# Score, level and first accumulator pairs in two-bank tiles, with two banks each for projections and the rest, in a hybrid mixer kernel

## The chip, the cores and the metric

The kernel runs on one core of a Trainium2 chip. The metric is the device time of one execution in microseconds. Three runs of the kernel before gave 436.5, 437.03 and 437.03 us, so the median is 437.03 us.

## The reference

One layer works on 128 context rows and 512 latent rows, 640 rows of width 1024 in all. They are RMS-normalised, scaled and shifted by vectors that come from a conditioning product, and sent through one input projection. The projected columns feed three groups of heads, each of which is multiplied by a SiLU gate. Then come one output projection, an RMSNorm, a gate and the residual. Cut to what matters here:

```python
h = rmsnorm(x, g_pre) * (1 + scale) + shift          # scale, shift, gate = silu(c) @ w_ada + b_ada
qa, ka, va, ga, qr, zf, zb, ir, gr, uf, gf = split(h @ w_in)
# A: 8 heads of 64; a latent row reads its 8 x 16 window and 256 cached context keys, with a bias
s = concat([q @ k_window.T * scale + bias, q @ k_ctx.T * scale])
oa = softmax(s) @ concat([v_window, v_ctx])
# B: 4 heads of 64, forward and backward gated recurrence, written in chunks
o = (q * exp(G)) @ state + (decayed q @ k.T, causal) @ v
# C: Re(2-D DFT over positions and group channels) @ w_fnet
mixed = concat([oa * silu(ga), rmsnorm(o_r) * silu(gr), o_f * silu(gf)])
y = x + gate * rmsnorm(mixed @ w_out, g_post)
```

## The kernel before

Everything is laid out with columns of the model on the partitions and the 640 rows along the free side. Products in 32-bit precision are made as three products of a high and a low part (`split`, lines 126 to 128, writes a high part on ScalarE and a low part on VectorE).

The stages are generators, each of which yields when it would wait, and a small clock (`Order`, lines 39 to 68) interleaves them into one program. The framework then schedules that program against a simulated time line (`TCKW`, line 36). For each engine it takes, of the instructions whose inputs and buffers are ready, the one that stands earliest in the program. The order that comes out is fixed at build time, and on the chip each engine works through its own list and waits on semaphores. `issue_after` and `add_manual_dep` add edges that keep one instruction behind another.

The stages around the change are these.

- **Start** (`start_stream`, 242 to 279; `zf_stream`, 281 to 292). For each of eight k, `mod_cols` (192 to 198) makes 16 small products with 32 output columns each, in four column groups, into a tile `pm`. They are turned by `tr`, summed, and give scale and shift; `modulated` (231 to 240) turns the rows of x into the tile `px` and applies them. The projections `zf0` and `zf1` run along as the k arrive, into four accumulators `zf_acc` (206), and `gate` (319 to 327) reads them.
- **Projections** (`block`, 297 to 312). Each of the other blocks of 128 columns is made in two halves of 320 rows. One half is 24 products of 320 columns into one accumulator `acc`, which a `use` function then reads on ScalarE or VectorE. The block `ir` is made by `token_blocks` (348) with products of 256 columns.
- **Recurrence** (`recurrence`, 414 to 551), twice. Seven levels each make, in `level` (431 to 450), eight and then two products of 64 contraction rows. The two heads of a pair sit on the upper and the lower 64 rows, and their products alternate between two accumulators `pa`. VectorE copies them out under a mask (450). After the levels come the tiles `pd`, `pk`, `pst` and the two output accumulators `po` (529).
- **Attention** (`attention`, 637 to 776), four times, each with four latent tiles and one context tile. `scores` (641 to 647) makes a run of products of 64 contraction rows. In a latent tile that is six against the cached keys (names `kc` and `tqs`) and six against the window's keys (`tks` and `tqs`), alternating between two accumulators `pss`, one for each head of the pair. In the context tile it is six of 128 columns. The softmax, the turned probabilities (`transposes`, tile `ptr`), and the weighted sums (`weighted`, `context_rest`) follow.
- **Gate vectors** (`gate_vectors`, 844 to 876). Eight times 8 products through `mod_cols` into `pm`, read by a `split`, and four times four products into `pg`, read on VectorE in line 875.
- **Fourier and output** (`fourier`, 798; `out_first`, 895; `out_second`, 919). Five accumulators `pz`, then `pf`, then the output projection over four banks at once and one more, then its second half.

PSUM has eight accumulator tiles ("banks" here) of 512 columns. `PB(tag)` (105) takes one from a tag: `b` has five and `f` three (`WB`, 27). Projections take `f`, as do the single-bank part of `by_token` (343), `pm` and `pg` of the gate vectors, `pz`, `pf`, `pw` and the second half of the output projection. All else takes `b`. Of `zf_acc` three banks are `f` and one is `b`. The first half of `zb0` takes `b`.

The alternating order of a run is held by `follow` (115 to 120): every product of a run gets an edge to the one before it. The edge keeps the order, but lets other products in between. The two accumulators of a pair are two tiles, and a product can be scheduled when its own tile is free:

```python
pss, pes, chain = [PB(), PB()], [], []
...
for hh in (1, 0):
    follow(chain, mm(outs[hh], qs[a][RS[hh], cols], keys(b)[RS[hh]], start=(n == 0), stop=(n == 2)))
```

Of the kernel before, what the change touches and what calls it, by code (L numbers as in the profile page):

```python
# [9 lines left out]
F32 = mybir.dt.float32  # L10
# [7 lines left out]
P = 128  # L18
# [8 lines left out]
WB = {"raw": 2, "hi": 3, "lo": 3, "t": 18, "pe": 2, "o": 4, "cf": 3, "pb": 5, "pf": 3, "s": 8, "m": 4, "row": 2, "tbl": 1, "pT": 8, "vs": 2, "kc": 4}  # L27
# [44 lines left out]
def mixer_kernel(ctx: ExitStack, tc: tile.TileContext, A, O):  # L72
# [34 lines left out]

    last_tr = [None]
# [6 lines left out]
    def follow(chain, ins):  # L115

        if chain:
            tc.add_manual_dep(ins, chain[-1].name, mybir.DependencyInfo(mybir.DependencyClass.NoSync,
                                                                        mybir.DependencyReason.DATA), reason="turns")
        chain.append(ins)  # L120
# [71 lines left out]
    def mod_cols(out, w):  # L192

        t = od.now
        for k in range(KT):
            o = out[32 * (k % 4):32 * (k % 4) + 32, :]
            mm(o, csil[:, k, :], w[:, k, :], start=(k < 4), stop=(k >= 4))
        od.now = t + 0.45
# [7 lines left out]
    zf_w, zf_acc = [], [[PB("f"), PB("f")], [PB("f"), PB()]]  # L206
# [35 lines left out]
    def start_stream():  # L242
# [13 lines left out]
        for k in range(KT):  # L256
# [3 lines left out]
            pm = PB()  # L260
            for u in range(2):
                mod_cols(pm[:, u * P:(u + 1) * P], raws[2 * k + u])
# [34 lines left out]
    def block(name, use, lo_eng=ve):  # L297

        w = load_w(A["win"][BLOCKS.index(name)], lo_eng)
        for u in range(2):  # L300
            acc = PB("bf"[u] if name == "zb0" else "f")[:, 0:320]
# [112 lines left out]
    def recurrence(p):  # L414
# [16 lines left out]
        def level(KB, QB, li):  # L431
# [3 lines left out]
            for i0, i1 in ((0, 4), (4, 5)):  # L435
                pa = [PB(), PB()]
                t, chain = od.now, []
                for i in range(i0, i1):
                    for hh in (1, 0):
                        ins = mm(pa[hh][:, (i - i0) * P:(i - i0 + 1) * P], KB[RS[hh], i * P:(i + 1) * P],  # L440
                                 QB[RS[hh], i * P:(i + 1) * P])
                        follow(chain, ins)
# [86 lines left out]
        po = PB(), PB()  # L529
# [107 lines left out]
    def attention(p):  # L637
# [3 lines left out]
        def scores(outs, qt, keys, chain):  # L641

            cols, t = slice(qt * P, (qt + 1) * P), od.now
            for n, (a, b) in enumerate(((0, 0), (0, 1), (1, 0))):
                for hh in (1, 0):
                    follow(chain, mm(outs[hh], qs[a][RS[hh], cols], keys(b)[RS[hh]], start=(n == 0), stop=(n == 2)))
# [4 lines left out]
        def softmax_context():  # L651
            pss, pes = [PB(), PB()], []
# [16 lines left out]
        def softmax_latent(qt):  # L669
            pss, pes, chain = [PB(), PB()], [], []  # L670
# [127 lines left out]
    def fourier():  # L798
# [28 lines left out]
        for u in range(2):  # L827
            pf = PB("f"), PB("f")
# [15 lines left out]
    def gate_vectors():  # L844
        selr = cp.tile([P, 2, P], F32R, tag="selr", name="selr")
        gp.tensor_copy(selr, sel)
        for q in range(8):
# [16 lines left out]
            mod_cols(pm[:, 0:P], w)  # L864
# [30 lines left out]
    def out_first():  # L895
# [8 lines left out]
        banks = [PB() for _ in range(4)]  # L904
# [7 lines left out]
        banks.append(PB("b" if WB["pb"] > 4 else "f"))  # L912
# [216 lines left out]
```

## Time and profile before

| | before |
|---|---|
| median of 3 runs | 437.03 us |
| the profiled execution's own time | 437.11 us |
| its span | 435.3 us |
| granted TensorE clock, mean over the span | 0.996 |
| VectorE busy | 303.5 us (70%) |
| ScalarE busy | 205.8 us (47%) |
| mean DMA rate | 109 GB/s |

The span goes from the first to the last instruction of one execution on the chip, and 1.8 us of that execution's time lie outside it. In the views, PE is TensorE's products, PEld its weight loads, DVE is VectorE and ACT is ScalarE. A row of the time line gives the start, the length of the stretch, the engine, the line, what is written and read, the shape and the count. Products overlap in TensorE's pipeline, so what a product costs is the step from its start to the next one's start, and not its length. An accumulator has the name `pb`, whatever its tag. A product of 64 contraction rows shows as 64*128, and one of `mod_cols` as 128*32. A full 32-bit product shows as two instructions.

### The profile page before, as it was taken

How to read it: one execution, taken by the hardware profiler on the slowest of the kernel's cores; microseconds unless marked ns; L12 is line 12 of the kernel's file. 1: busy time of each engine (PE TensorE's matmuls, PEld its weight loads, DVE VectorE, ACT ScalarE, POOL GpSimd, SP SyncE). 2: the span in 40 equal slices, each digit the busy share in tenths (PEclk: the TensorE clock that was granted, in tenths of full speed). 3: DMA queues.
4: the chain of work that ended last, by engine and by line, in shares of the span. 5: the costliest groups of instructions: out<-in, count | busy, mean ns of one | idle time of the engine just before them, and what ended most of it. 6: DMA issues, size and time to landing. Idle time of an engine off the chain costs nothing.

```text
span 435.3 us, 8309 instructions
## 1 busy us (share of the span) xinstructions
PE 411.3 (94%) x3176; PEld 372.7 (86%) x3176; DVE 303.5 (70%) x866; ACT 205.8 (47%) x546; POOL 7.4 (2%) x23
## 2 busy tenths in 40 slices
PE   0699999999998999999999999999999999999994
PEld 0488899999988998999899889889898988988884
DVE  2775479999986866885597658885768928670174
ACT  6434467565341526654444444753556643350161
POOL 2000000000020100000000000000000000000000
PEclk9999999999999999999999999999999999999998
DMA  7996153211302021122021413245134302481023
GB/s 236 412 407 229 49 158 114 74 45 50 88 20 76 10 62 48 56 97 74 32 68 60 145 50 104 98 147 163 51 119 150 96 0 66 140 291 48 0 105 139
DMA packets 19528, 47.62 MB, mean 109 GB/s; under 512 B 3184, under 2 KB 6912, under 8 KB 19488
## 3 DMA queue, kind: packets, MB, share of 16 engines
q1 hardware_dynamic: 19376, 46.94, 32.0%
q8 instruction: 25, 0.41, 0.4%
q0 software_dynamic: 112, 0.14, 0.3%
q14 instruction: 15, 0.12, 0.1%
HBM read 43.80 MB, written 3.28 MB: 108 GB/s over the span
## 4 chain that ended last, share of the span: by engine, by line
PE 90%; DVE 3%; DMA 3%; ACT 1%; issue 1%; SPq 0%; DVEq 0%; ACTq 0%
PE pb L113 84%; PE pb L124 7%; DMA vs<-wss 2%; DMA txa<-x 1%; DVE AL L450 1%; DVE t L524 1%; DVE AL L487 0%; ACT L679 0%; DVE t L951 0%; ACT pe L680 0%; DVE t L467 0%; DVE t L466 0%; DVE AC L450 0%; DVE t L468 0%; SPq L190 0%
## 5 line engine op out<-in xcount | busy, mean ns | idle before, releaser
L113 PE MATMUL pb<-hT,hi 128*128 128x320 f32 x896 | 208.7, 317 | 2.5 <-DVE vs L128 1.5
L113 PEld LDWEIGHTS pb<-hT,hi 128*128 128x128 f32 x896 | 148.7, 188 | 9.0 <-issue 3.3
L113 PE MATMUL pb<-hT,lo 128*128 128x320 f32 x448 | 139.1, 312 | 0.0
L113 PEld LDWEIGHTS pb<-hT,lo 128*128 128x128 f32 x448 | 84.0, 188 | 1.3 <-DVE G L272 0.2
L128 DVE TENSOR_TENSOR lo<-raw,hi 128x1024 fp32r<-128x1024 f32 x35 | 42.8, 1223 | 18.7 <-ACT hi L127 18.5
L127 ACT CAST hi<-raw 128x1024 fp32r<-128x1024 f32 x35 | 36.8, 1050 | 28.4 <-PE pb L113 17.5
L113 PE MATMUL pb<-t,t 64*128 64x128 f32 (+2 forms) x414 | 42.9, 291 | 0.4 <-DVE AL L450 0.4
L113 PEld LDWEIGHTS pb<-t,t 64*128 64x128 f32 (+1 forms) x414 | 36.0, 188 | 4.7 <-issue 0.7
L127 ACT CAST pT<-pb 128x256 fp32r<-128x256 f32 x64 | 23.5, 373 | 22.3 <-DVE pT L128 11.1
L113 PE MATMUL pb<-hi,mh 128*128 128x512 f32 (+1 forms) x108 | 30.8, 375 | 0.0
L128 DVE TENSOR_TENSOR pT<-pb,pT 128x256 fp32r<-128x256 f32 x64 | 26.5, 419 | 1.7 <-ACT pT L127 1.5
L679 ACT ACTIVATE pe<-pb,s 128x256 f32<-128x256 f32 x32 | 15.3, 478 | 17.5 <-DVE s L678 8.4
L113 PEld LDWEIGHTS pb<-hi,mh 128*128 128x128 f32 x108 | 19.6, 188 | 3.7 <-DVE mh L128 0.3
L113 PE MATMUL pb<-pT,mh 128*128 128x512 f32 (+1 forms) x102 | 21.9, 364 | 0.0
L124 PE MATMUL pb<-ident,pe 128*128 128x128 f32 x136 | 21.0, 274 | 0.5 <-ACT pe L680 0.5
L113 PEld LDWEIGHTS pb<-pT,mh 128*128 128x128 f32 x102 | 17.7, 189 | 3.1
L113 PE MATMUL pb<-lo,mh 128*128 128x512 f32 (+1 forms) x54 | 19.5, 375 | 0.0
L934 ACT ACTIVATE t<-pb 128x512 f32<-128x512 f32 (+1 forms) x11 | 6.1, 552 | 26.9 <-PE pb L113 26.7
L690 DVE TENSOR_TENSOR o<-pb,o 64x512 f32<-64x512 f32 (+1 forms) x16 | 7.8, 486 | 15.5 <-ACT o L689 15.4
L124 PEld LDWEIGHTS pb<-ident,pe 128*128 128x128 f32 x136 | 16.5, 140 | 1.7 <-ACT pe L680 0.7
L450 DVE COPY_PREDICATED AL<-masks,pb 128x512 f32<-128x512 uint32 x24 | 16.6, 742 | 1.7 <-PE pb L113 1.6
L113 PE MATMUL pb<-pT,vs 128*128 128x256 f32 (+1 forms) x96 | 17.0, 320 | 0.0
(205 smaller groups left out, 635.3 us busy)
## 6 DMA issues: line engine op xcount, KB each, us to landing
raw<-win SPq DMA_DIRECT2D x30, 512.0 KB, 3.5
pT<-wss SPq DMA_DIRECT2D x12, 512.0 KB, 10.3
raw<-wg SPq DMA_DIRECT2D x8, 512.0 KB, 3.6
raw<-wout SPq DMA_DIRECT2D x8, 512.0 KB, 3.6
t<-x SPq DMA_DIRECT2D x10, 256.0 KB, 5.4
o_y<-t SPq DMA_DIRECT2D x9, 256.0 KB, 2.2
vs<-wss SPq DMA_DIRECT2D x4, 512.0 KB, 9.5
tbl<-tbl SPq DMA_DIRECT2D x4, 512.0 KB, 3.5
```

Of the source, the lines that this page charges most:

```text
L113: return te.matmul(out, lhsT, rhs, start=start, stop=stop).ins
L124: last_tr[0] = te.transpose(out, src, ident).ins
L127: (sc.copy if hi_eng is None else hi_eng.tensor_copy)(hi, src)
L128: (ve if lo_eng is None else lo_eng).tensor_sub(lo, src, hi.bitcast(F32))
L450: ve.copy_predicated(out, mk.to_broadcast([P, i1 - i0, P]), src)
L524: ve.scalar_tensor_tensor(sall[r, cdst], sall[r, cs], Td[r, ip:ip + 1], pst[r, cdst], op0=ALU.mult, op1=ALU.add)
L679: sc.activation(pe[:, 256:512], ss[:, 256:512], ACT.Exp, bias=m[:, 1:2], accum_out=m[:, 3:4])
L690: ve.tensor_add(out, src[r, :], out)
L934: sc.activation(T(512)[:, cs], po[:, 0:cs.stop - cs.start], ACT.Square, accum_out=ssb[:, j:j + 1])
```

## The change

- The tags become `b` with two banks, `f` with two, and `s` with two tiles of two banks each (`PB2`). The sum is still eight banks.
- `s` holds the score pairs `pss`, the level pairs `pa`, the output pair `po` of the recurrence, `zf_acc`, and the first four accumulators of the output projection. Such a tile is taken and given back as one.
- `pm` of the start moves from `b` to `f`, the first half of `zb0` from `b` to `f`, and one `pf` of the Fourier stage from `f` to `b`.
- `run_mm` takes the place of `follow`. It keeps the edges, and it makes every product of a run but its first inside `tc.high_priority()`, which lets the scheduler see it as if it stood at the start of the program. `mod_cols` makes its products through it too, each call with a chain of its own.

```diff
-WB = {..., "pb": 5, "pf": 3, "s": 8, ...}
+WB = {..., "pb": 2, "pf": 2, "ps": 2, "s": 8, ...}
...
+    def PB2():
+
+        t = ps.tile([P, 2, 512], F32, tag="s", name=nm("ps"), bufs=WB["ps"])
+        return [t[:, j, :] for j in range(2)]
...
-    def follow(chain, ins):
-
+    def run_mm(chain, *args, **kw):
+
+        with tc.high_priority() if chain else ExitStack():
+            ins = mm(*args, **kw)
         if chain:
             tc.add_manual_dep(ins, chain[-1].name, ...)
         chain.append(ins)
...
-    def mod_cols(out, w):
+    def mod_cols(out, w, chain):
...
-            mm(o, csil[:, k, :], w[:, k, :], start=(k < 4), stop=(k >= 4))
+            run_mm(chain, out[32 * (k % 4):32 * (k % 4) + 32, :], csil[:, k, :], w[:, k, :], start=(k < 4), stop=(k >= 4))
...
-    zf_w, zf_acc = [], [[PB("f"), PB("f")], [PB("f"), PB()]]
+    zf_w, zf_acc = [], [PB2(), PB2()]
...
-            pm = PB()
+            pm = PB("f")
...
-            acc = PB("bf"[u] if name == "zb0" else "f")[:, 0:320]
+            acc = PB("f")[:, 0:320]
...
-                pa = [PB(), PB()]
+                pa = PB2()
...
-        po = PB(), PB()
+        po = PB2()
...
-            pss, pes, chain = [PB(), PB()], [], []
+            pss, pes, chain = PB2(), [], []
...
-            pf = PB("f"), PB("f")
+            pf = PB("f"), PB()
...
-        banks = [PB() for _ in range(4)]
+        banks = PB2() + PB2()
```

The products themselves, their number and their operands stay as they are.

More of the change, by code (lines that the diff above doesn't have):

```diff
@@ L26 @@
 TOKENS = ("ir",)
-WB = {"raw": 2, "hi": 3, "lo": 3, "t": 18, "pe": 2, "o": 4, "cf": 3, "pb": 5, "pf": 3, "s": 8, "m": 4, "row": 2, "tbl": 1, "pT": 8, "vs": 2, "kc": 4}
+WB = {"raw": 2, "hi": 3, "lo": 3, "t": 18, "pe": 2, "o": 4, "cf": 3, "pb": 2, "pf": 2, "ps": 2, "s": 8, "m": 4, "row": 2, "tbl": 1, "pT": 8, "vs": 2, "kc": 4}
 RAW = ["vs", "pT", "pT", "pT"] * 4
@@ L190, in load @@
             sy.dma_start(t, src)
-    def mod_cols(out, w):
+    def mod_cols(out, w, chain):
         t = od.now
         for k in range(KT):
-            o = out[32 * (k % 4):32 * (k % 4) + 32, :]
-            mm(o, csil[:, k, :], w[:, k, :], start=(k < 4), stop=(k >= 4))
+            run_mm(chain, out[32 * (k % 4):32 * (k % 4) + 32, :], csil[:, k, :], w[:, k, :], start=(k < 4), stop=(k >= 4))
         od.now = t + 0.45
@@ L259, in start_stream @@
             row = sp.tile([P, 256], F32, tag="AC", name=nm("row"), bufs=2)
-            pm = PB()
+            pm = PB("f")
             for u in range(2):
-                mod_cols(pm[:, u * P:(u + 1) * P], raws[2 * k + u])
+                mod_cols(pm[:, u * P:(u + 1) * P], raws[2 * k + u], [])
             yield 0
@@ L439, in level @@
                     for hh in (1, 0):
-                        ins = mm(pa[hh][:, (i - i0) * P:(i - i0 + 1) * P], KB[RS[hh], i * P:(i + 1) * P],
-                                 QB[RS[hh], i * P:(i + 1) * P])
-                        follow(chain, ins)
+                        run_mm(chain, pa[hh][:, (i - i0) * P:(i - i0 + 1) * P], KB[RS[hh], i * P:(i + 1) * P],
+                               QB[RS[hh], i * P:(i + 1) * P])
                 od.now = 0.5 * (t + od.now)
@@ L645, in scores @@
                 for hh in (1, 0):
-                    follow(chain, mm(outs[hh], qs[a][RS[hh], cols], keys(b)[RS[hh]], start=(n == 0), stop=(n == 2)))
+                    run_mm(chain, outs[hh], qs[a][RS[hh], cols], keys(b)[RS[hh]], start=(n == 0), stop=(n == 2))
             od.now = 0.5 * (t + od.now)
@@ L651, in softmax_context @@
         def softmax_context():
-            pss, pes = [PB(), PB()], []
+            pss, pes = PB2(), []
             scores([t[:, 0:P] for t in pss], 0, lambda b: ks[b][:, 0:P], [])
@@ L863, in gate_vectors @@
             pm, es = PB("f"), slice(q % 2 * P, q % 2 * P + P)
-            mod_cols(pm[:, 0:P], w)
+            mod_cols(pm[:, 0:P], w, [])
             split(pm[:, 0:P], *[t[:, es] for t in rows])
@@ L911, in out_first @@
                 yield 0
-        banks.append(PB("b" if WB["pb"] > 4 else "f"))
+        banks.append(PB())
         for n, k in enumerate(kord):
```

## The prediction

> **What bounds the kernel now.** I read the page first, then TensorE's waits, then the busy time by stretches, and last the time line of TensorE row by row. Times below are those of the profiled execution, 437.11 us, of which 435.3 us are its span; the median of the runs is 437.03 us, so the two differ by less than 0.1 us and the sum can be read against either. A change of less than 0.2%, 0.9 us, could not be told from none.
>
> ```profile
> span 435.3 us, 8309 instructions
> PE 411.3 (94%) x3176; PEld 372.7 (86%) x3176; DVE 303.5 (70%) x866; ACT 205.8 (47%) x546; POOL 7.4 (2%) x23
> ```
>
> ```profile
> PE pb L113 <- DMA vs<-wss: 14.5, 1, 14.5
> PE pb L113 <- DVE vs L128: 1.5, 1, 1.5
> PE pb L113 <- ACT t L324: 1.0, 1, 1.0
> ```
>
> ```profile
> 120.00:134.00 14.00, 12.18 (x114) 10.72 (x110) 12.92 (x40) 6.23 (x16) 2.42 (x6) 1.00 0.04 11
> ```
>
> ```profile
> 245.00:345.00 100.00, 100.00 (x796) 89.56 (x795) 75.44 (x243) 54.61 (x168) 0.00 (x0) 1.00 0.34 107
> ```
>
> TensorE is the bound. After the first loads have come (14.5 us) its named waits are 1.5 and 1.0 us, and in 245 to 345 us it is busy for all of the 100 us while VectorE has 75.44 and ScalarE 54.61. In one stretch, 120 to 134, VectorE is nearly full (12.92 of 14) and TensorE is not (12.18). Time is won here only by making TensorE's list shorter, and lost wherever TensorE has nothing that it may start.
>
> A busy TensorE is not a well used one. This is one latent tile's run of twelve products of 64 rows as it now stands:
>
> ```profile
> 177.15 0.38 PE L113 MATMUL pb<-kc,tqs 64*128 64x256 f32 x1
> 177.46 0.41 PE L113 MATMUL pb<-hT,hi 128*128 128x320 f32 x1
> 177.71 0.30 PE L113 MATMUL pb<-hT,lo 128*128 128x320 f32 x1
> 177.85 0.45 PE L113 MATMUL pb<-hT,hi 128*128 128x320 f32 x2
> 178.14 0.30 PE L113 MATMUL pb<-hT,lo 128*128 128x320 f32 x1
> 178.38 0.61 PE L113 MATMUL pb<-kc,tqs 64*128 64x256 f32 x5
> 178.72 0.62 PE L113 MATMUL pb<-tks,tqs 64*128 64x256 f32 x6
> 179.27 0.56 PE L113 MATMUL pb<-hT,hi 128*128 128x320 f32 x2
> ```
>
> The run's first product stands alone, five projection products follow, and then come the other eleven. This is one of the few runs that stand whole:
>
> ```profile
> 225.24 0.62 PE L113 MATMUL pb<-kc,tqs 64*128 64x256 f32 x6
> 225.69 0.51 PE L113 MATMUL pb<-tks,tqs 64*128 64x256 f32 x6
> 226.14 0.41 PE L113 MATMUL pb<-hT,lo 128*128 128x320 f32 x1
> ```
>
> Read the steps between starts. The whole run takes 226.14 - 225.24 = 0.90 us for twelve products, so two of different halves run at the same time. In the cut run the lone first takes 177.46 - 177.15 = 0.31, and the other eleven 179.27 - 178.38 = 0.89, nearly what all twelve need. Inside a row of projections a product costs (178.14 - 177.71) / 3 = 0.143 us, about 0.145. The first one after the lone product costs 177.71 - 177.46 = 0.25, which is 0.10 more, and the last one ahead of the eleven costs 178.38 - 178.14 = 0.24, which is 0.09 more: the change between forms costs at both ends. So the cut costs 0.31 + 0.10 + 0.09 + 0.89 - 0.90 = 0.49 us.
>
> **The change part by part.** *Scores.* Where a run's second product writes another bank than its first, it can be held back until that bank is free, and the scheduler fills the hole with projections. With one tile for both banks the run starts when both are free, and what follows has priority over every projection, so no hole is left. The lone firsts in the time line are 14 of the 20 runs. The first is the one above and the last is this:
>
> ```profile
> 337.77 0.32 PE L113 MATMUL pb<-tks,tqs 64*128 64x128 f32 x1
> ```
>
> 14 x 0.49 = 6.9 us. Four of them are context tiles with narrower products, which may be worth 0.05 less each. All lie beyond 167 us, where the stretch quoted shows TensorE full, so all of it is on the path.
>
> *Gate vectors and start.* Runs of `mod_cols` are cut too. Six times the 16 instructions of a run stand in two pieces; a cut one, and a whole one for comparison:
>
> ```profile
> 245.25 0.42 PE L113 MATMUL pb<-raw,csil 128*32 128x128 f32 x6
> 245.60 0.66 PE L124 MATMUL pb<-ident,pe 128*128 128x128 f32 x4
> 246.18 0.62 PE L113 MATMUL pb<-raw,csil 128*32 128x128 f32 x10
> 246.74 0.56 PE L113 MATMUL pb<-hT,hi 128*128 128x320 f32 x2
> ```
>
> ```profile
> 270.75 0.64 PE L113 MATMUL pb<-raw,csil 128*32 128x128 f32 x16
> 271.33 0.56 PE L113 MATMUL pb<-hT,hi 128*128 128x320 f32 x2
> ```
>
> The pieces take 245.60 - 245.25 = 0.35 and 246.74 - 246.18 = 0.56, the whole run 271.33 - 270.75 = 0.58: 0.33 lost, and with the changes of form (up to 0.10 + 0.09 above, less where a piece stands beside another run) between 0.33 and 0.52. I take 0.4; 6 x 0.4 = 2.4 us.
>
> *Levels.* Three of the 28 runs of the recurrence have a lone first, as here:
>
> ```profile
> 128.79 0.48 PE L113 MATMUL pb<-t,t 64*128 64x128 f32 x2
> 129.20 0.56 PE L113 MATMUL pb<-hT,hi 128*128 128x320 f32 x2
> ```
>
> 129.20 - 128.79 = 0.41, with 0.10 + 0.09 about 0.6 us each. This one lies in the stretch 120 to 134 where TensorE has time to spare and is worth nothing. The other two (at 77 and 137 us) lie where it is full: 1.2 us.
>
> *First accumulators.* The 1.0 us wait for `t` L324 is the second half of `zb0`, which needs an `f` bank that a `zf` accumulator still holds. Those accumulators move to `s`, and `pm` has long left `f` by then, so this wait goes: 1.0 us. That `pm` now has two banks of its own where it had shared four with `px` costs nothing as long as `zb0` does not start before the last k; it now starts after it.
>
> The sum of what goes: 6.9 + 2.4 + 1.2 + 1.0 = 11.5 us.
>
> *What is given back.* Projections are the filler of every hole, and they have two banks for three. An accumulator takes 24 x 0.145 = 3.5 us to fill. Three places show the third bank at work.
>
> First, at 104 to 147 us the readers of the projections are late behind the recurrence, and TensorE fills three banks ahead of them; the 1.5 us wait in the table above is for the third. With two banks, one accumulator's worth, 3.5 us, can't be done ahead. Against that stands this row:
>
> ```profile
> 120.54 1.34 DVE L450 COPY_PREDICATED AL<-masks,pb 128x512 f32<-128x512 uint32 x2 [1.64 <-PE pb L113]
> ```
>
> VectorE, the bound there, sits idle 1.64 us for a level run that is queued behind projections of just that third accumulator. Without them the level comes earlier. I take 3.5 - 1.6 = 1.9, about 2.0, between 0 and 3.5.
>
> Second, the four `pg` tiles of the gate vectors sit in an `f` bank until VectorE has read them:
>
> ```profile
> 266.35 0.52 PE L113 MATMUL pb<-row,selr 128*128 128x256 f32 x3
> 266.70 0.46 PE L113 MATMUL pb<-hT,hi 128*128 128x320 f32 x2
> ```
>
> ```profile
> 267.75 0.33 ACT L598 COPY t<-pb 128x192 f32<-128x192 f32 x1
> ```
>
> While this `pg` waits, the next half block starts at 266.70 in the third bank. With two, it must wait until the last half is read at 267.75 + 0.33 = 268.08, 1.4 us later. The other three would wait 1 us or less, so 0 to 4 us in all. Turned probabilities and scores are there to fill half of it: 2.0.
>
> Third, the Fourier stage:
>
> ```profile
> 344.36 0.54 PE L113 MATMUL pb<-hT,hi 128*128 128x320 f32 x2
> ```
>
> ```profile
> 365.78 0.76 ACT L331 ACTIVATE tg<-pb 128x320 f32<-128x320 f32 x2
> ```
>
> ```profile
> 357.61 0.59 ACT L806 COPY t<-pb 128x512 f32<-128x512 f32 x1 [0.77 <-PE pb L113]
> ```
>
> The half block `ga2` begun at 344.36 isn't read before 365.78. The five `pz` in that time then have one bank in place of two, and each of the last four must wait for the copy (0.59 us, with the signals about 1.0): 0 to 4 us. The weighted sums of the last attention and the first products of the output projection are at hand to fill it, so I take 1.0.
>
> Given back: 2.0 + 2.0 + 1.0 = 5.0, between 0 and 3.5 + 4 + 4 = 11.5.
>
> The Trainium skill speaks against a price for the third bank: "TensorE: Matmul & The Clock Gate", section "HAM oscillation", tells of a kernel, with its loop already put in order, that gained nothing more from double-buffering PSUM. By that rule the give-back would be 0, and the sum 425.6. The 1.5 us wait of this trace says otherwise for this kernel, whose readers are late.
>
> *Pairs given back as one.* A pair's first bank now stays taken until the second is read. Before, two pairs and a single bank shared the five of `b`; now two pairs have four, and `ptr`, `po` and the rest have two more. I cost this at nothing: the next run is no bound while other products stand ready. If none do, each of the 16 latent runs could wait for the second head's reading, about as long as a row above (0.3 to 0.6 us).
>
> The sum: 437.1 - 11.5 + 5.0 = 430.6 us.
>
> **The rivals.** *The whole saving is kept.* Attention fills all that the third bank filled: 437.1 - 11.5 = 425.6. For it speaks that the attention has more banks than before; against it, the 1.5 us wait.
>
> *Slower: projections starve.* Besides projections, 27 tiles use `f` from the recurrence to the Fourier stage (8 `pm`, 4 `pg`, 6 from `by_token`, 2 `pw`, 5 `pz`, 2 `pf`; one of the `pf` leaves). While one of them sits in a bank, projections have one bank, and TensorE stands still from the end of a half block until it is read. A gate's reading is 0.76 / 2 = 0.38 us on ScalarE and one on VectorE:
>
> ```profile
> 308.02 0.49 DVE L332 SCALAR_TENSOR_TENSOR tg<-tg,pb 128x320 f32<-128x320 f32 x1 [0.25 <-ACT tg L331]
> ```
>
> Together 0.9 us, 27 x 0.9 = 24.3 us if nothing fills. Half of that, 12.2, would use up the saving; if six in ten are uncovered, it is 14.6 and the time 437.1 - 11.5 + 14.6 = 440.2. It decides when over 11.5 / 24.3 = 47% stay uncovered. For it: the wait at 134 us and the late readers. Against it: beyond 150 us each such moment has other products in the list.
>
> *The runs stay cut.* If what holds the second product is not its bank (keys that are not yet split, a transposition that the scheduler has placed already), the 6.9 and 1.2 stay, and 437.1 - 2.4 - 1.0 + 5.0 = 438.7. Against it: the operands of a run's first two products are of the same tiles, ready together. Where the keys are late, in the first two runs at 159 us, the cut will stay; that isn't counted above.
>
> *The clock falls.* More short waits could lower TensorE's granted clock, which is 1.00 in both stretches above, even where it idles 1.8 of 14 us; at the very end, with nothing to do, it shows less:
>
> ```profile
> 430.00:435.30 5.30, 0.00 (x0) 0.00 (x0) 1.96 (x5) 0.22 (x1) 0.00 (x0) 0.67 0.29 101
> ```
>
> At 0.67, the 12.18 us of work in 120 to 134 would take 18.2, 6.0 more: 436.6. The Trainium skill's "TensorE: Matmul & The Clock Gate", section "A second HAM failure mode: psum-queue depth-cycling", states that short idles between groups as PSUM banks are cycled make the clock oscillate. By that, the trace would already have to show it in 120 to 134, and it doesn't.
>
> **How the numbers follow.** The forecast, most of the saving with a part given back, has 0.55, with 426 to 436 as its own range. The whole saving kept: 0.12. Starved projections: 0.20. Runs that stay cut: 0.10. The clock: 0.03. The range goes from 425.5, the whole saving, to 440.5, the starved case; worse starving is left out, as is a saving beyond the count. Faster by over 0.2% (below 436.2): 0.55 less 0.03 for its upper end, plus 0.12, is 0.64. Within 0.2%: that 0.03, the clock's 0.03 and 0.03 of the cut runs, 0.09. Slower: 0.20 and 0.07 of the cut runs, 0.27.
>
> **What would show it.** The time line after should have 12 products of `tqs` in a row for each latent tile, 6 for each context tile, 16 instructions in each `mod_cols` run, with lone firsts gone but for the first tiles at about 159 us. The wait for `t` L324 should be gone from TensorE's list. Given-back time should show as idle TensorE with ScalarE or VectorE reading an accumulator as its releaser, near 114 to 134, at the `pg` tiles and in the Fourier stage. Wrong would be: runs whole and TensorE's idle time up by more than 11 us; runs still cut; or a saving from another place, such as VectorE's part of the recurrence.

## The result and the profile after

| | before | after |
|---|---|---|
| median of 3 runs | 437.03 us | 457.3 us (456.25 to 460.61) |
| the profiled execution's own time | 437.11 us | 460.61 us |
| its span | 435.3 us | 458.8 us |
| granted TensorE clock, mean over the span | 0.996 | 0.977 |

The changed kernel is slower: the ratio is 1.0484, with an interval from 1.0448 to 1.0521. The forecast was 430.6 us. From here on, a line number in the changed kernel is five to seven higher than the same line before (L118 is the old L113, L135 the old L128), and a tile of the tag `s` is named `ps`.

The page of after, its span, its busy times, and TensorE's busy share and granted clock in 40 slices of 11.5 us each:

```profile
span 458.8 us, 8338 instructions
PE 411.0 (90%) x3176; PEld 374.1 (82%) x3176; DVE 302.9 (66%) x866; ACT 204.3 (45%) x546; POOL 7.4 (2%) x23
PE   0799869999888889899999899989999898999994
PEclk9999979999987999999999999999999999999998
```

TensorE is busy as long as before, 411.0 against 411.3 us. Its idle time went from 435.3 - 411.3 = 24.0 to 458.8 - 411.0 = 47.8 us, and the 23.8 us of difference are the whole loss of this execution, the slowest of the three (the others had 456.25 and 457.3 us at a mean clock of 0.990 and 0.985). Shares under 9 now stand all over the span, where attention before had been full. What ended these pauses, in TensorE's list of waits, behind the 13.7 us at the very start (us in total, times, longest):

```profile
PE pb L118 <- ACT t L330: 4.9, 1, 4.9
PE ps L118 <- DVE AL L455: 3.1, 2, 2.2
PE pb L118 <- ACT tq L613: 2.9, 4, 1.2
PE pb L118 <- DVE t L880: 2.7, 2, 1.7
PE ps L118 <- DVE t L529: 2.0, 1, 2.0
PE pb L118 <- ACT t L811: 1.9, 3, 0.7
```

Most of these are products into `pb` held up by the reader of an accumulator: the gate of the start (L330, the old L324), queries (L613), a gate vector (L880, the old L875), the Fourier copy (L811, the old L806). The two rows of `ps` are the recurrence.

The whole runs that the forecast counted on are there at the same time. A latent tile's run in the time line of after:

```profile
191.52 0.62 PE L118 MATMUL ps<-kc,tqs 64*128 64x256 f32 x6
191.97 0.51 PE L118 MATMUL ps<-tks,tqs 64*128 64x256 f32 x6
192.42 0.66 PE L131 MATMUL pb<-ident,pe 128*128 128x128 f32 x4
```

Twelve products in a row, in 192.42 - 191.52 = 0.90 us. Counted over the whole time line, the 20 score runs stand in 22 pieces and not 36 (14 fewer, as many as forecast), the eight late runs of `mod_cols` in 8 and not 13, the levels, 14 times 20 products, in 14 and not 17.

Since the runs got shorter and TensorE's busy time did not, something made other work longer. Busy time by stretches has it (the columns are the bounds, the length, busy time and count of PE, PEld, DVE, ACT and POOL, the granted clock, the DMA share and rate):

```profile
60.80:65.20 4.40, 4.40 (x16) 4.40 (x17) 3.32 (x6) 1.53 (x3) 0.00 (x0) 0.50 0.43 129
134.40:139.60 5.20, 5.20 (x19) 4.97 (x19) 4.91 (x14) 1.00 (x3) 0.00 (x0) 0.50 0.00 2
147.30:150.60 3.30, 3.30 (x18) 3.30 (x18) 0.00 (x0) 0.00 (x0) 0.00 (x0) 0.50 0.46 163
260.00:345.00 85.00, 81.73 (x678) 74.58 (x677) 61.87 (x205) 43.72 (x141) 0.00 (x0) 1.00 0.32 100
```

In the first three, TensorE works without a pause at a clock of 0.50. These 4.40 + 5.20 + 3.30 = 12.9 us of work would have taken little over half as long at 1.00 (a product takes 0.267 us and not 0.146, in the rows at the end of this document), so some 6 us were lost there. The fourth is in attention: it idles 85.00 - 81.73 = 3.3 us, in a stage that had no idle time before. Its clock is 1.00.

By events of the time line, the loss is spread in time as well. The first level product comes 5.4 us late. From there to the last one the recurrence takes 73.7 us and not 68.4, and from there to the first context tile of attention 56.2 and not 51.6. Attention between its first and last context tile is 2.6 us shorter, but from the last context tile to the end it takes 108.5 us and not 97.6. (A context tile counts here from its first score product.)

### The profile page after: what moved, and what is told of

Same layout as the page of the kernel before. It is cut to its first block, busy times and chain, and to the rows that moved or that the text cites. A ratio compares the mean times of both kernels' runs of the same rounds, so it can differ in the third digit from the quotient of the medians.

```text
span 458.8 us, 8338 instructions
## 1 busy us (share of the span) xinstructions
PE 411.0 (90%) x3176; PEld 374.1 (82%) x3176; DVE 302.9 (66%) x866; ACT 204.3 (45%) x546; POOL 7.4 (2%) x23
## 4 chain that ended last, share of the span: by engine, by line
PE 71%; DVE 9%; DMA 8%; ACT 7%; issue 3%; SPq 1%; DVEq 0%; ACTq 0%
PE pb L118 52%; PE ps L118 15%; DMA raw<-win 5%; PE pb L131 4%; ACT hi L134 2%; DVE lo L135 2%; DMA raw<-wout 1%; DMA txa<-x 1%; DVE t L529 1%; DVE AL L455 1%; DMA cf<-kc 1%; SPq L197 1%; DVE pT L135 1%; ACT pe L685 0%; ACT t L330 0%
## 5 line engine op out<-in xcount | busy, mean ns | idle before, releaser
L118 PE MATMUL pb<-hT,hi 128*128 128x320 f32 x832 | 195.3, 320 | 16.8 <-ACT t L330 4.9
L118 PEld LDWEIGHTS pb<-hT,hi 128*128 128x128 f32 x832 | 141.6, 192 | 22.1 <-ACT t L330 5.2
L118 PE MATMUL pb<-hT,lo 128*128 128x320 f32 x416 | 131.1, 315 | 0.0
L118 PEld LDWEIGHTS pb<-hT,lo 128*128 128x128 f32 x416 | 79.8, 192 | 0.4
L135 DVE TENSOR_TENSOR lo<-raw,hi 128x1024 fp32r<-128x1024 f32 x35 | 42.7, 1221 | 35.0 <-ACT hi L134 34.9
L118 PE MATMUL ps<-t,t 64*128 64x128 f32 (+1 forms) x312 | 26.3, 290 | 2.9 <-DVE t L529 2.0
L118 PEld LDWEIGHTS ps<-t,t 64*128 64x128 f32 (+1 forms) x312 | 22.3, 194 | 5.5 <-DVE t L529 2.2
L135 DVE TENSOR_TENSOR pT<-pb,pT 128x256 fp32r<-128x256 f32 x64 | 26.1, 415 | 0.9 <-ACT pT L134 0.9
L684 ACT ACTIVATE pe<-ps,s 128x256 f32<-128x256 f32 x32 | 15.2, 475 | 12.1 <-DVE s L683 4.1
L455 DVE COPY_PREDICATED AL<-masks,ps 128x512 f32<-128x512 uint32 x24 | 16.3, 732 | 4.9 <-PE ps L118 4.9
L118 PE MATMUL pb<-t,t 128*128 128x128 f32 (+1 forms) x102 | 17.2, 314 | 2.5 <-ACT t L505 1.3
L131 PE MATMUL pb<-ident,txa 128*128 128x128 f32 x25 | 5.7, 324 | 14.4 <-DVE txa L234 13.7
L118 PEld LDWEIGHTS pb<-t,t 128*128 128x128 f32 x102 | 14.1, 190 | 4.7 <-ACT t L505 1.8
L680 DVE TENSOR_REDUCE s<-ps 128x1 f32<-128x256 f32 x32 | 13.1, 417 | 6.1 <-ACT pe L684 4.3
L118 PE MATMUL pb<-hi,mh 128*128 128x512 f32 (+1 forms) x60 | 16.8, 363 | 0.0
L118 PE MATMUL pb<-pT,vs 128*128 128x256 f32 (+1 forms) x96 | 16.7, 322 | 0.0
L118 PE MATMUL pb<-pT,mh 128*128 128x512 f32 (+1 forms) x78 | 16.6, 357 | 0.0
L118 PE MATMUL ps<-hT,hi 128*128 128x320 f32 x64 | 16.4, 329 | 0.2 <-DVE hT L244 0.2
```

What stands on the lines that cost most here:

```text
L118: return te.matmul(out, lhsT, rhs, start=start, stop=stop).ins
L131: last_tr[0] = te.transpose(out, src, ident).ins
L135: (ve if lo_eng is None else lo_eng).tensor_sub(lo, src, hi.bitcast(F32))
L455: ve.copy_predicated(out, mk.to_broadcast([P, i1 - i0, P]), src)
L680: ve.reduce_max(m[:, 0:1], ss[:, 256:512], axis=AX.X)
L684: sc.activation(pe[:, 256:512], ss[:, 256:512], ACT.Exp, bias=m[:, 1:2], accum_out=m[:, 3:4])
```

## The experiments

The theory was this: whole runs save about what was forecast, and the division of the eight banks among the tags costs more than that. Which part of the division, was open: fewer banks for projections, 27 small tiles in them, pairs that are given back as one, or the six other banks cut in four and two. Rivals: that the priority upsets the schedule, and that the clock is the cause and not a consequence. Each comparison below was made against the kernel before on the same chip, which had medians of 436.3 to 436.9 us there.

### Third projection bank

Two kernels made of the one before, without pairs and without priority, with six banks `b` and two `f`. In the first all four `zf_acc` are `b`, in the second two are:

```diff
-WB = {..., "pb": 5, "pf": 3, ...}
+WB = {..., "pb": 6, "pf": 2, ...}
-    zf_w, zf_acc = [], [[PB("f"), PB("f")], [PB("f"), PB()]]
+    zf_w, zf_acc = [], [[PB(), PB()], [PB(), PB()]]                 # two_f
+    zf_w, zf_acc = [], [[PB("f"), PB("f")], [PB(), PB()]]           # two_f_plain
```

> The kernel before with only the banks recounted: six single banks for the rest, two for projections, the four first accumulators and nothing else moved out of the projections' tag; no pairs in one tile, no priority. Theory S (two projection banks starve TensorE): idle time of TensorE after its first product rises from 3.5 us to 20 or more, the clock falls for some us, time 452 to 467 us with the runs still cut. Rival P (pairs given back as one hold up scores and levels) and rival Q (priority upsets the order): 435 to 441 us, idle time under 8 us.

> The kernel before with six single banks for the rest and two for projections; two first accumulators stay in the projections' tag and two go to the other, so that the start is as free as before. No pairs, no priority. If the third projection bank is the cause beyond the start: 445 to 460 us, with 10 to 25 us of idle TensorE from the recurrence on. If the slow time of the recount run before this came from the start, where it left one bank for the scale and shift tiles: 436 to 441 us.

Measured: two_f 456.14 us, 1.0439 [1.0415, 1.0463]; two_f_plain 443.68 us, 1.0167 [1.0124, 1.0209]. Two accumulators of the start in the one tag or the other are worth about 12 us, more than the third bank is; which wait makes that difference isn't shown here. In two_f_plain the third bank costs 0.0167 x 437 = 7.3 us, after what the rest gains from a sixth. The page of two_f_plain:

```profile
span 444.7 us, 8296 instructions
PE 414.0 (93%) x3176; PEld 375.1 (84%) x3176; DVE 300.9 (68%) x866; ACT 205.1 (46%) x546; POOL 7.3 (2%) x23
```

444.7 - 414.0 = 30.7 us idle, 6.7 more than before, which is most of the 9.4 us by which this span is longer. By events of the time line it lies at the end: 110.9 us from the last context tile on, before 97.6. The projection products (those that read `hT`) from the last score product to the end, before and in two_f_plain (bounds, length, then busy time and count of PE and PEld):

```profile
343.30:435.30 92.00, 14.85 (x96) 14.26 (x96) 0.00 (x0) 0.98 0.30 99
334.00:444.70 110.70, 22.62 (x144) 21.24 (x144) 0.00 (x0) 0.97 0.28 97
```

144 of the 1464 are left for the end and not 96. At the forecast's 0.145 us each, 48 more are 7.0 us, an estimate that is about the whole cost: projections that were not made ahead are made there.

### Back to three, at the cost of one of the rest

The changed kernel with three banks for projections, one for the rest, and the two pairs:

```diff
-WB = {..., "pb": 2, "pf": 2, "ps": 2, ...}
+WB = {..., "pb": 1, "pf": 3, "ps": 2, ...}
```

> The changed kernel with three banks for projections and one for the rest; pairs and priority stay. Theory S: the idle time falls back towards 5 us, the runs stay whole, and the time is 426 to 434 us, unless the one bank left for transposes and weighted sums binds in its turn. Rival P: 450 us or more, as the pairs are still there. Rival Q: 450 us or more, as the priority is still there.

Measured: 521.91 us, 1.1966 [1.1929, 1.2003]. TensorE's waits name the one bank of `b`, in which turned probabilities wait to be split (L135) and which the turning of the next ones needs, late behind the softmax (L683):

```profile
PE pb L131 <- DVE pT L135: 21.0, 9, 3.1
PE pb L131 <- DVE s L683: 9.6, 5, 2.6
```

So the third projection bank isn't to be had this way, and the banks of the rest are dear too: the second of them is worth over 60 us, even against a third for projections.

### Priority alone, and everything but priority

```diff
+    def run_mm(chain, *args, **kw):                                 # priority_only: the kernel before
+        with tc.high_priority() if chain else ExitStack():          # with these calls, its banks kept
...
-        with tc.high_priority() if chain else ExitStack():          # no_priority: the kernel after
+        with ExitStack():
```

> The kernel before with the priority for a run's products but its first, and the chain in the scale and gate products; all tiles and banks as before. Theory S: no starving, idle time about 3.5 us; the score runs are still cut after their first product if it is the second bank that is missing, the cuts of the scale and gate products go, 433 to 437 us. Rival P: the same. Rival Q: 445 us or more.

> The changed kernel without the priority: the order within a run is kept, tiles and banks as changed. Theory S: as slow as the changed kernel or a little slower, 455 to 465 us, with idle time over 20 us. Rival P: the same. Rival Q: 435 to 442 us. If the cuts come back although both banks of a run come free at once, it was the priority and not the tile that closed them; if they stay away, it was the tile.

Measured: priority_only 435.44 us, 0.9966 [0.9953, 0.998]; no_priority 460.93 us, 1.0541 [1.0498, 1.0584]. The priority isn't the cause of the loss. Nor does it close the score runs by itself. The time line of priority_only, at the run that the forecast quoted:

```profile
177.09 0.38 PE L113 MATMUL pb<-kc,tqs 64*128 64x256 f32 x1
177.40 0.41 PE L113 MATMUL pb<-hT,hi 128*128 128x320 f32 x1
```

The first product stands alone as before; 37 pieces for 20 runs. In no_priority it is 25, so other banks close the runs, and the second product's bank was indeed what it waited for. But a tile of two banks isn't needed for that: two_f_plain, with six single banks, has 28 pieces, and split42 below, with four single banks of their own for the pairs and no priority, has 25. What priority_only closes are the `mod_cols` runs, 8 pieces and not 13.

### The 27 other tiles out of the projections' banks

two_f_plain, with `pm`, `pg`, `pz`, `pf`, `pw` and the tiles of `by_token` moved to `b`, so that the two `f` are left to projections:

```diff
-        pt = PB(), PB("f")
+        pt = PB(), PB()
...
-            pm, es = PB("f"), ...
+            pm, es = PB(), ...
```

> As two_f_plain, and the 27 other tiles of the projections' tag (gate vectors, transposed blocks, Fourier) take one of the six banks of the rest, so that the two are for projections alone. Theory S1 (those 27 take the place of a projection): 434 to 440 us. Theory S2 (two accumulators are not enough for the projections themselves, since their readers come late): within 4 us of two_f_plain.

Measured: 449.91 us, 1.0322 [1.028, 1.0363], slower than two_f_plain by 6 to 7 us. The waits of f_alone have turned up on the other side, before the turning of probabilities (L124), and the clock falls among them (a row by stretches):

```profile
PE pb L124 <- ACT pe L680: 4.6, 4, 1.9
```

```profile
263.76:280.83 17.07, 12.68 (x74) 9.23 (x72) 14.21 (x57) 10.42 (x40) 0.00 (x0) 0.50 0.10 33
```

12.68 us of work at 0.50 lose some 6 us, nearly the whole difference. No projection product starts between 259.6 and 285.7 us. At 259.9 us f_alone has made 1032 of them, two_f_plain 1003, so they were made a little earlier and were missing where softmax had to be covered. What was missing were their weights. The loads of weights go in order through two buffers `raw`, and the next load waits for the first product of the gate vectors, which comes at 279.41 us, in two_f_plain at 254.1 and before at 245.25:

```profile
229.61 0.33 SPq L175 DMA_DIRECT2D raw<-wg  x1
279.41 1.08 PE L113 MATMUL pb<-raw,csil 128*32 128x128 f32 x16
280.56 0.33 SPq L175 DMA_DIRECT2D raw<-win  x1
```

The accumulator of that product, `pm`, is one of the tiles that were moved to `b`. That it came late for want of a bank there is likely, but not shown. So this run doesn't tell what the 27 tiles cost the projections: moving them out made a new wait.

### The wait at the start

The longest wait of after is at 60.80 us. Its row in TensorE's time line, and ScalarE's rows ahead of it:

```profile
60.80 0.90 PE L118 MATMUL pb<-hT,hi 128*128 128x320 f32 x2 [4.93 <-ACT t L330]
```

```profile
55.11 1.28 ACT L329 ACT_TABLE_LOAD   x1
56.40 0.44 ACT L329 ACTIVATE t<-ps 128x320 f32<-128x320 f32 x1
...
57.69 1.07 ACT L134 CAST hi<-raw 128x1024 fp32r<-128x1024 f32 x1
...
59.90 0.51 ACT L329 ACTIVATE t<-pb 128x320 f32<-128x320 f32 x1
```

Both halves of `zb0` are full at about 55.9 us and hold both `f` banks. ScalarE reads the four `zf` accumulators ahead of them, with a table load and casts between, and reaches the first half of `zb0` at 59.90. Then the first half goes back to a bank `b`, as before the change:

```diff
-            acc = PB("f")[:, 0:320]
+            acc = PB("bf"[u] if name == "zb0" else "f")[:, 0:320]
```

> The changed kernel with the first half of zb0 in a bank of the rest, as before the change. The wait of 4.9 us at 60.8 us, with 6.8 us of half clock behind it, came from both halves of zb0 filling both projection banks while ScalarE had four other pairs to read first. If that is so, the wait shrinks below 2 us, the first half-clock stretch goes, and the time is 449 to 454 us. If the wait is ScalarE's alone: 456 to 459 us.

Measured: 455.07 us, 1.0436 [1.0401, 1.0472]. Waits of 0.69 and 1.56 us stand in place of the 4.93, in the time line of zb0_b:

```profile
56.89 0.41 PE L118 MATMUL pb<-hT,lo 128*128 128x320 f32 x1 [0.69 <-DVE lo L135]
61.95 0.57 PE L118 MATMUL pb<-hT,hi 128*128 128x320 f32 x2 [1.56 <-ACT t L330]
```

The stretch at half clock behind it is gone too. That is 4.93 - 0.69 - 1.56 = 2.7 us of waiting and some 2 us of the 4.4 us of work. The ratios, 1.0436 against 1.0484, make it a gain of about 2 us, with intervals that allow anything from none to 4. Whether a part of the pause is made up later isn't shown.

### Pairs given back as one

The changed kernel with four single banks `s` in place of two pairs (singles), and one with three `f`, three `b` and one pair, in which the levels' short runs take two `b` (one_pair):

```diff
-        t = ps.tile([P, 2, 512], F32, tag="s", name=nm("ps"), bufs=WB["ps"])     # singles
-        return [t[:, j, :] for j in range(2)]
+        return [ps.tile([P, 512], F32, tag="s", name=nm("ps"), bufs=4) for _ in range(2)]
```

```diff
-WB = {..., "pb": 2, "pf": 2, "ps": 2, ...}                                       # one_pair
+WB = {..., "pb": 3, "pf": 3, "ps": 1, ...}
-                pa = PB2()
+                pa = PB2() if i0 == 0 else [PB(), PB()]
```

> The changed kernel with its s tag made of four single banks in place of two tiles of two; the tags, who takes which, and the priority are as changed. If a pair being taken and given back as one is what costs 15 us over two_f_plain: 440 to 448 us, with the score runs cut again after their first product. If the narrow partition (two banks each for projections and the rest) is what costs: 455 to 465 us, with the cuts back and the idle time as in the changed kernel.

> Three projection banks and three for the rest as single tiles, and one tile of two banks for scores, the eight products of a level, the recurrence's output pair and two of the output projection's accumulators; priority as in the change. Start and first accumulators as before the change. Theory S: projections do not starve, the runs stand whole, idle TensorE under 8 us, 426 to 433 us. Rival P (a pair given back as one holds up the next run): the single pair holds up every latent tile, 440 us or more, with idle time at the scores.

Measured: singles 461.25 us, 1.0573 [1.0542, 1.0605]; one_pair 455.48 us, 1.0419 [1.0368, 1.047]. Freeing each bank by itself makes it slower than after, by about 4 us (2 to 6), with 25 pieces of score runs and not 22. That a pair is given back as one isn't what costs. With one pair TensorE waits in other places, five times 1.1 us at the start and once behind the softmax:

```profile
PE pb L118 <- ACT t L241: 5.5, 5, 1.1
PE pb L131 <- DVE pe L688: 3.9, 1, 3.9
```

### Six banks cut in four and two

two_f_plain, with the six `b` divided: four single banks `s` for `pss`, `pa`, `po`, two of `zf_acc`, the first half of `zb0`, `pm` and the output's four, and two `b` for the rest. No pairs, no priority:

```diff
-WB = {..., "pb": 6, "pf": 2, ...}
+WB = {..., "pb": 2, "pf": 2, "ps": 4, ...}
-                pa = [PB(), PB()]
+                pa = [PB("s"), PB("s")]
...
-        po = PB(), PB()
+        po = PB("s"), PB("s")
```

> As two_f_plain, with its six banks of the rest divided as in the changed kernel: four single ones for scores, levels, the recurrence's output, two first accumulators and the output projection, and two for all else; the scale and shift tiles take the four. No pairs, no priority, the start as before the change. If the division of the rest is what the changed kernel loses beyond the projections' bank: 450 to 457 us, with the last level of the recurrence at 144 us or later (138.3 in two_f_plain). If it is the start or the priority: 442 to 446 us and the last level before 141 us.

Measured: 466.71 us, 1.069 [1.0666, 1.0714]: 23 us more than two_f_plain, for a dividing line and nothing else, although its score runs stand in 25 pieces and not 28. The stretch from the first level product to the last has over half of it. Four kernels in this stretch, two_f_plain (six banks for all), before (five), after (two pairs and two) and split42 (four and two), each by its own view:

```profile
75.40:139.80 64.40, 64.28 (x575) 57.32 (x575) 60.37 (x158) 32.59 (x78) 4.20 (x12) 1.00 0.15 48
```

```profile
74.20:144.10 69.90, 68.08 (x629) 62.93 (x628) 62.60 (x162) 34.30 (x82) 4.33 (x12) 1.00 0.18 56
```

```profile
79.60:154.80 75.20, 68.82 (x618) 64.36 (x618) 61.23 (x161) 33.49 (x82) 4.32 (x12) 0.93 0.17 52
```

```profile
73.50:151.60 78.10, 74.55 (x621) 66.91 (x620) 62.75 (x166) 34.97 (x84) 3.98 (x12) 0.96 0.13 40
```

VectorE (the third busy column) has 60 to 63 us of work in each. With six banks for all it fills the stretch but for 64.40 - 60.37 = 4.0 us; in split42, 78.10 - 62.75 = 15.4 us are idle. What VectorE waits for in split42 is this:

```profile
DVE s L541 <- ACT t L540: 8.5, 1, 8.5
DVE AL L450 <- PE pb L113: 5.9, 3, 2.7
```

and in after, the same two lines, five further on:

```profile
DVE s L546 <- ACT t L545: 7.2, 1, 7.2
DVE AL L455 <- PE ps L118: 4.9, 3, 1.9
```

The first is the end of one recurrence, which runs late; the kernel before has this wait too, with 4.9 us, and two_f_plain with 2.6. The second are level runs that come late. The forecast meant to win such a wait, of 1.64 us at 120.54 us, the only one before; there are three now, and more of it.

### Where in the division

Three changes to split42: `pd`, `pk` and `pst` of the recurrence to `s` (rec_s); `po` to `b` (po_b); and the levels' short runs to `b`, so that the levels have all six banks (lvl6):

```diff
-        pd = PB()                                                                # rec_s; pk, pst likewise
+        pd = PB("s")
-        po = PB("s"), PB("s")                                                    # po_b
+        po = PB(), PB()
-                pa = [PB("s"), PB("s")]                                          # lvl6
+                pa = [PB("s"), PB("s")] if i0 == 0 else [PB(), PB()]
```

> split42 with the recurrence's pd, pk and pst in the four banks of scores and levels, so that the two banks of the rest hold nothing of the recurrence but the transposed output. If it is the two banks of the rest that make the recurrence late: the stretch from its first to its last level falls from 77 us to 63 to 68, and the time to 446 to 456 us. If it is the four banks, or the output pair in them: 70 us or more, 462 to 470 us.

> split42 with the recurrence's output pair in the two banks of the rest in place of the four. VectorE's wait of 8.5 us for the square of that output, which stands in its list ahead of the last levels, shrinks if the pair came late for want of one of the four: under 5 us, the level stretch 65 to 70 us, time 450 to 458 us. If the pair is not what holds it: within 4 us of split42.

> This is split42 with the levels' short runs (two products) moved from the four banks of s to the two of b; their long runs (eight products) stay in s. If the division cost its time because all the level runs of the recurrence share four banks in place of six, the level stretch (76.6 us from the first level product to the last in split42, 62.9 with six banks undivided) comes down to 63 to 68 us, and the time to 450 to 456 us. If the levels' banks are not what holds it (the products of the next level wait for VectorE whatever banks they have, or the stretch is longer because less other work is left for the holes), the stretch stays at 73 us or more and the time within 4 us of split42's 466.71.

Measured: rec_s 466.68 us, 1.0705 [1.0679, 1.0731]; po_b 463.12 us, 1.0618 [1.0593, 1.0643]; lvl6 459.88 us, 1.0519 [1.0491, 1.0547]. rec_s changes nothing and po_b 3 to 4 us. So either the recurrence's own small tiles don't crowd the two-bank tag, or what that tag gains the four banks lose. lvl6 wins about 7 us and shortens the stretch (from the first level product to the last) from 76.6 to 68.4 us, in both less than was expected of it if the levels' banks were the cause.

So the banks of the levels are some 30% of the 23 us. The other 16 us are not in one place. In lvl6 TensorE idles 9.0 us between the first and the last score product of a latent tile, where two_f_plain idles 2.5, and from the last context tile to the end it takes 116.0 us against 110.9, with 169 projection products left behind the last score product and not 144. Which tile holds it up there wasn't settled.

### Fewer lines, not more

If dividing costs, joining could win. merged4 is after with `b` and `f` joined in one tag of four; all8 is priority_only with all eight banks in one tag:

```diff
-        return ps.tile([P, 512], F32, tag=tag, name=nm("pb"), bufs=WB["p" + tag])
+        return ps.tile([P, 512], F32, tag="b", name=nm("pb"), bufs=WB["pb"])
```

> The changed kernel with its two banks for projections and two for the rest joined into one tag of four; pairs and priority as changed. If the partition binds: 438 to 450 us, the runs whole, idle TensorE under 15 us. If the pairs cost: 453 to 460 us.

> The kernel before with the priority for runs and all eight banks in one tag as single tiles. If it is the freedom of the banks that counts: 428 to 435 us, nothing partitioned. If projections, being always ready, take banks that the recurrence and the scores need: 440 us or more, with idle time or late scores.

Measured: merged4 484.89 us, 1.1114 [1.1074, 1.1154]; all8 469.09 us, 1.075 [1.0684, 1.0816]. Both are worse. The level stretch of all8 is the shortest of all, 62.6 us, but then this stands in TensorE's waits, first of merged4 and then of all8:

```profile
PE pb L131 <- DVE pe L688: 21.1, 15, 3.6
```

```profile
PE pb L126 <- DVE pe L683: 7.5, 5, 2.9
PE pb L126 <- DVE s L681: 5.4, 4, 2.5
```

All are softmax steps of attention with nothing to cover them. It isn't that projections, with free use of the banks, were made early and used up. From the last score product to the end all8 still makes 200 of them (merged4 196, before 96):

```profile
351.80:464.90 113.10, 32.40 (x200) 29.70 (x200) 0.00 (x0) 0.98 0.31 104
```

There was filler left, and it wasn't made where softmax had to be covered. In all8, as in f_alone, the first product of the gate vectors comes late, at 284.7 us, and the next projection's weights are asked for only behind it, at 285.4. Whether that, or banks held by others, kept the projections back wasn't settled. In the kernel before, three banks for projections and five for the rest do not only hold data: they also keep some banks for the filler.

### What is left of the change

The kernel before, with the edges and the priority in `mod_cols` alone:

```diff
-    def mod_cols(out, w):
+    def mod_cols(out, w, chain):
...
-            mm(o, csil[:, k, :], w[:, k, :], start=(k < 4), stop=(k >= 4))
+            run_mm(chain, out[32 * (k % 4):32 * (k % 4) + 32, :], ..., hp=True)
```

> The kernel before with chain and priority in the scale and gate products alone; runs of scores and levels as before, all tiles and banks as before. The six cuts of those products go: about 2 us of TensorE, no new idle time, 434 to 436 us, the fastest of all. If the priority moves other work as much as it saves: 436 to 438 us.

Measured: 435.34 us, 0.9962 [0.9949, 0.9975], faster than both kernels, and with the shortest span:

```profile
span 434.0 us, 8311 instructions
PE 408.9 (94%) x3176; PEld 372.1 (86%) x3176; DVE 303.4 (70%) x866; ACT 205.1 (47%) x546; POOL 7.4 (2%) x23
```

TensorE's busy time goes from 411.3 to 408.9 us, its idle time from 24.0 to 25.1.

## Why the prediction was wrong

The kernels make a ladder from before to after. A step's cost is the difference of the ratios, times 437 us:

| step | ratio to before | step's cost |
|---|---|---|
| third projection bank given up, for a sixth of the rest (two_f_plain) | 1.0167 | +7.3 us |
| six others cut in four and two (split42) | 1.069 | +22.9 us |
| priority, and the tiles of the start and one `pf` moved as in the change (singles) | 1.0573 | -5.1 us |
| four `s` as two tiles of two banks (after) | 1.0484 | -3.9 us |

The intervals of the ratios are 0.002 to 0.004 to either side, so a step is known to about 2 us.

**The saving: right in mechanism, not shown in size.** Score runs: 14 lone firsts were forecast gone, and there are 14 pieces fewer. That a bank held the second product was right, since priority without other banks leaves the runs cut. `mod_cols`: 2.4 us were forecast for six cuts; alone, with the six closed, it brings 0.38% [0.25, 0.51], 1.7 us (1.1 to 2.2). For scores and levels no run gives the price by itself. The last two rungs give 9.0 us, near the 11.5 of the forecast, but this is no proof of it: the score runs are down to 28 and 25 pieces already on the rungs above. An estimate goes by TensorE's busy time: 411.0 us less the 6 that the half clock added is 405, 6 less than before, where the terms that are work (6.9 + 2.4 + 1.2) came to 10.5. The first two runs, at 171 us now, stay cut, as said: their products against the cached keys come well ahead of those against the window's. One later run, from 306 to 319 us, stands in three pieces.

**First accumulators: wrong.** The 1.0 us wait for `t` L324 was to go. It became one of 4.9 us, since the move of `zb0`'s first half to `f` puts both its halves in the projections' two banks. The forecast said that `zb0` now starts after the last k and costs nothing, and didn't ask when its readers are done with the four accumulators ahead of it. With the first half in `b` the wait is 1.56 us; about 2 us come back, not clear of none.

**The third bank: the size was about right, the first place not.** 5.0 us were forecast (0 to 11.5), 7.3 measured (5.4 to 9.1), and that the two are near is in part luck. It isn't lost at 104 to 147 us, where the stretch even gets shorter (64.40 us against 69.90 in the rows above): it is lost at the end, where the work is made up that was not made ahead. The other two places show in the waits of after: 2.7 us at the `pg` tiles (L880) and 1.9 at the Fourier copies (L811), where 2.0 and 1.0 were forecast.

The Trainium skill tells of one kernel that, once its loop was put in order, gained nothing more from double-buffering PSUM ("TensorE: Matmul & The Clock Gate", section "HAM oscillation"); that doesn't carry over to this kernel, where the third of three banks is worth 7.3 us.

**The step that failed** is "Pairs given back as one", with its words that "`ptr`, `po` and the rest have two more", costed at nothing (`po` is attention's own tile of that name here). Measured, the division of the six banks costs 22.9 us, over four times all that the forecast gave back. It isn't the pairing itself, which wins 3.9 us. Two things were wrong with the step. The banks were counted by kind of user and not by who may borrow from whom: with all six banks for the levels (lvl6) 7 of the 22.9 us come back. And the cover named for it ("other products stand ready") isn't always there: in lvl6 TensorE idles 9.0 us in attention, where it idles 2.5 in two_f_plain. Why the cover fails there is open.

The forecast had named this outcome as one that would make it wrong: runs whole, and idle time up by more than 11 us. It is up by 23.8.

**The rivals.** "Projections starve" had the right sign and the right kind of symptom, TensorE idle behind a reader, but not the price: two_f_plain leaves all 27 tiles in two banks with the projections and loses 7.3 us in all (at most 9.1), though with a sixth bank for the rest, where 14.6 were named. Its mechanism isn't tested by itself, as f_alone brought a new wait. "The runs stay cut" falls with the counts above, and "the whole saving is kept" with the time.

**The clock** had 3 in 100, as a case by itself. It is part of the loss here, as a consequence: work done at 0.50 took some 6 us more than at 1.00, in three stretches, each at pauses. In the 4.93 us wait it is at 1.00 up to 58.45 us and at 0.50 from 58.50 on; at 134 us it falls in the second of two waits of 0.73 and 0.82 us on both sides of ten products of two columns:

```profile
132.27 1.28 PE L118 MATMUL pb<-bones,t 128*128 128x2 f32 x10 [0.73 <-DVE t L529]
134.37 0.87 PE L118 MATMUL pb<-hT,hi 128*128 128x320 f32 x2 [0.82 <-DVE vs L135]
```

In the kernel before, a wait of 1.5 us at the same place leaves it at 1.00. What the Trainium skill says of short idles between groups ("TensorE: Matmul & The Clock Gate", section "A second HAM failure mode: psum-queue depth-cycling") fits the second place: this trace agrees with it, with 0.50 granted over 5.2 us, though no experiment here took these pauses away by themselves. The first place went with its pause (zb0_b).

**What stays open** is where some 16 of the 23 us of the division arise. The levels' banks are about 7; for the rest the views show 6.5 us more of idle time in attention and an end that is 5.1 us longer, and three kernels that moved one kind of tile each did not find a single cause.

## What to carry to other kernels

A pool of buffers is also the ration of each stage: before dividing one, list for every stage which tiles it borrowed from the common stock at its busiest, and not how many tiles of each kind there are. When the order is found by a scheduler, work that can go anywhere is a stock to cover waits. Fewer buffers for it push it to the end, and so can buffers that all may take; its own inputs, such as weights that are still to be loaded, can keep it from a wait as well. Count in the time line how much of it is left at the end of each stage. Where an edit joins a gain (closed runs) with a new division of buffers, try the two apart: here the closed `mod_cols` runs alone win 0.4%, and the whole edit loses 4.8%.

## What the runs showed of the hardware

TensorE's clock went to 0.50 in stretches of 3 to 7 us in after and over 17 us in f_alone, and a projection step took 1.8 times as long there. In the rows of after from 61.76 to 64.96 us, twelve products take 3.20 us, 0.267 each; a little later nine take 1.31 us, 0.146 each:

```profile
61.76 0.73 PE L118 MATMUL pb<-hT,hi 128*128 128x320 f32 x2
...
64.96 0.62 PE L118 MATMUL pb<-hT,hi 128*128 128x320 f32 x2
...
65.57 0.45 PE L118 MATMUL pb<-hT,hi 128*128 128x320 f32 x2
...
66.88 0.31 PE L118 MATMUL pb<-hT,hi 128*128 128x320 f32 x1
```

The mean over the span, 0.977, hardly tells of it: a pause of 4.9 us costs about another 2 us behind it, and it is seen only in the clock of that stretch.
